# Batched matrix product on one core: the rounding to 16 bits moved to GpSimd, VectorE and ScalarE in loops, one output buffer per group

## The chip, the core and the metric

The kernel runs on one core of one Trainium2 chip. The metric is the device time of one execution in microseconds (us); lower is better. Each kernel is run several times and the median counts. Beside the times there is a profile: one execution recorded by the hardware profiler, with the start and length of each instruction on the engines TensorE (PE in the profile; its weight loads are PEld), VectorE (DVE), ScalarE (ACT), GpSimd (POOL) and SyncE (SP), and with the DMA transfers.

## What is computed

The reference is a batch of 32 independent matrix products in float32:

```
x: (32, 256, 512)   y: (32, 512, 384)   out: (32, 256, 384)
out = einsum('bij,bjk->bik', x, y)
```

x is 16.8 MB, y is 25.2 MB and the output is 12.6 MB, so 54.5 MB cross between the device memory and the core's SBUF.

## The kernel before

**Groups.** The 32 batches are worked through in N = 8 groups of Q = 4 batches. One DMA (`load_x`, lines 65 to 67) brings the four x of a group into `x_sb`: 32 partitions for each batch, 8 rows of 512 floats in each partition (16 KB). One DMA (`load_y`, lines 69 to 71) brings the four y into `y_sb`: again 32 partitions for each batch, 16 rows of 384 floats in each partition (24 KB). One DMA (`store`, lines 185 to 191) writes the output of a group. So a group has 5.24 MB of loads and 1.57 MB of stores. There are two buffers for x and three for y (lines 41 and 42).

**Rounding.** The products are made in float16. VectorE rounds x of a group in one instruction (`cast_x`, line 109, 4096 elements in each partition) into one of two `x_r` buffers, and y in four instructions of 1536 elements in each partition (`round_y`, line 124) into the single `y_r`.

**Transposes.** The products need x transposed. VectorE transposes pairs of float16 as if they were 32-bit words, in blocks of 32 by 32 (`transpose_x`, line 119). The output rows of a group are done in NE = 2 halves (e = 0 and 1), and the transposes of one half come in NC = 4 chunks, which go to the single buffer `xt_sb`. From group 6 on (`WIDE_GROUPS`) each chunk is two smaller transposes, and an output copy covers 64 partitions instead of 32.

**Products.** TensorE loops over groups and halves (lines 233 to 251). A half has T = 16 steps of four products, one for each batch of the group, each of 32 rows against 384 columns; the four batches use four row strips of the array and add up in four banks of PSUM, so there are eight banks for the two halves. TensorE waits for one `s_xt` mark for each chunk of four steps, and at the start of a half for the marks `s_act` and `s_dve`, which say that the banks have been copied out. `s_pe` counts what TensorE has finished: `chunk_done` is the mark of a chunk and `bank_done` that of a bank.

**Copies out of PSUM.** ScalarE copies seven of the eight banks of a group to SBUF and VectorE one, in pieces of 32 partitions (`collect`, line 137); in the last group they share the banks evenly. The outputs of groups 0 to 4 go to five `o_sb` buffers, those of groups 5 and 6 to the two halves of the third y buffer, and that of group 7 to the first `o_sb` buffer again, once the store of group 0 has landed (`s_first`).

**Order.** Each engine's order is written out by hand. VectorE does, for each group: the four transposes of half 1 (each after the chunk of half 0 is done), the rounding of the next x, then by turns a piece of the next y and a transpose of half 0 of the next group, then its copies. SyncE issues all DMAs, in program order, on one queue: y(0), x(0), y(1), x(1), then for n from 2 to 7 y(n) and x(n), and only then the eight stores (lines 193 to 204). y(n) waits until group n-3 has passed its half 0 (so that the third buffer back is free), x(n) until x(n-2) is rounded. Store n waits until the first chunk of half 1 of group n+1 is done; the last one waits for the last copies (`s_last`). GpSimd only clears semaphores at the end.

Of the kernel before, what the change touches and what calls it, by code (L numbers as in the profile page):

```python
# [8 lines left out]
MM_DT = mybir.dt.float16  # L9
F32 = mybir.dt.float32  # L10
P = 128
Q = 4
STEP = 4
WIDE_GROUPS = 6


@with_exitstack
def kernel(
# [6 lines left out]
    nc = tc.nc  # L25

    B, I, J = x.shape
    _, _, K = y.shape

    PQ = P // Q  # L30
    R = I // PQ
    T = J // PQ
    TW = T // 2
    NE = I // P
    N = B // Q
    NC = T // STEP

    def sbuf(name, shape, dtype):
        return nc.alloc_sbuf_tensor(name, shape, dtype).ap()

    x_sb = [sbuf(f"x_sb{i}", [P, R, J], F32) for i in range(2)]
    y_sb = [sbuf(f"y_sb{i}", [P, T, K], F32) for i in range(3)]
    o_sb = [sbuf(f"o_sb{i}", [P, R, K], F32) for i in range(5)]
    x_r = [sbuf(f"x_r{i}", [P, R, J], MM_DT) for i in range(2)]
    xt_sb = sbuf("xt_sb", [P, TW, P], F32)
    y_r = sbuf("y_r", [P, T, K], MM_DT)
    o_ps = nc.alloc_psum_tensor("o_ps", [P, NE * Q, 512], F32).ap()


    s_x = [nc.alloc_semaphore(f"s_x{n}") for n in range(N)]  # L50
    s_y = [nc.alloc_semaphore(f"s_y{n}") for n in range(N)]
    s_first = nc.alloc_semaphore("s_first")
    s_xt = nc.alloc_semaphore("s_xt")
    s_act = nc.alloc_semaphore("s_act")
    s_dve = nc.alloc_semaphore("s_dve")
    s_pe = nc.alloc_semaphore("s_pe")
    s_cast = nc.alloc_semaphore("s_cast")
    s_last = nc.alloc_semaphore("s_last")
    s_sp = nc.alloc_semaphore("s_sp")
    s_out = nc.alloc_semaphore("s_out")  # L60
    mine = s_x + s_y + [s_first, s_xt, s_act, s_dve, s_pe, s_cast, s_last, s_sp]
    nums = sorted(s.num for s in mine)
    assert nums == list(range(nums[0], nums[-1] + 1)) and s_out.num == nums[-1] + 1

    def load_x(n):
        src = x[n * Q : (n + 1) * Q].rearrange("g (p r) j -> (g p) r j", r=R)
        return nc.sync.dma_start(out=x_sb[n % 2], in_=src).then_inc(s_x[n], 16)

    def load_y(n):
        src = y[n * Q : (n + 1) * Q].rearrange("g (q t) k -> (g q) t k", t=T)  # L70
        return nc.sync.dma_start(out=y_sb[n % 3], in_=src).then_inc(s_y[n], 16)


    for ins in (load_y(0), load_x(0), load_y(1), load_x(1)):
        tc.no_tile_sem_insts.add(ins.ins.name)
    tc.close()
    tc.compile()  # L77


    MARKS = NC - 1 + Q  # L80

    def bank_done(n, e, g):
        return (n * NE + e) * MARKS + NC + g

    def chunk_done(n, e, a):
        return (n * NE + e) * MARKS + (a + 1 if a < NC - 1 else MARKS)

    def width(n):
        return PQ if n < WIDE_GROUPS else 2 * PQ

    def on_vector(n, e, g):
        if n < N - 1:
            return (e, g) == (NE - 1, Q - 1)
        return g % 2 == 1

    def o_of(n):
        if n in (5, 6):
            flat = y_sb[2].rearrange("p t k -> p (t k)")
            half = flat[:, (n - 5) * R * K : (n - 4) * R * K]
            return half.rearrange("p (r k) -> p r k", r=R)  # L100
        return o_sb[n % 5 if n < 5 else 0]


    v = nc.vector
    AW = STEP // 2

    def cast_x(n):
        v.wait_ge(s_x[n], 16)
        v.tensor_copy(x_r[n % 2], x_sb[n % 2]).then_inc(s_cast, 1)  # L109

    def transpose_x(n, e, a):
        b = width(n) // PQ
        src = x_r[n % 2].bitcast(F32).rearrange(
            "p (b h e) (q t) -> p b e t h q", b=b, e=NE, t=TW
        )
        dst = xt_sb.rearrange("p t (h s b) -> p b t h s", s=PQ, b=b)
        w = slice(a * AW, (a + 1) * AW)
        for c in range(b):
            ins = v.transpose(dst[:, c, w], src[:, c, e, w])  # L119
        ins.then_inc(s_xt, 1)  # L120

    def round_y(n, a):
        s = slice(a * STEP, (a + 1) * STEP)
        v.tensor_copy(y_r[:, s], y_sb[n % 3][:, s])  # L124

    def collect(n, eng, copy, vector, last):
        w = width(n)
        per = P // w
        o = o_of(n).rearrange("p (u f) k -> p u f k", u=Q // per)
        for e in range(NE):  # L130
            for g in range(Q):
                if on_vector(n, e, g) != vector:
                    continue
                eng.wait_ge(s_pe, bank_done(n, e, g))
                a = g % per * w
                for h in range(per):
                    ins = copy(  # L137
                        o[a : a + w, g // per, h * NE + e],
                        o_ps[h * w : (h + 1) * w, e * Q + g, :K],
                    )  # L140
                if (e, g) in last:
                    ins.then_inc(*last[e, g])


    v.sem_inc(s_dve, 3)
    v.wait_ge(s_y[0], 16)
    for a in range(NC):
        round_y(0, a)
    cast_x(0)
    v.wait_ge(s_cast, 1)  # L150
    for a in range(NC):
        transpose_x(0, 0, a)
    for n in range(N):
        for a in range(NC):
            v.wait_ge(s_pe, chunk_done(n, 0, a))
            transpose_x(n, 1, a)
        if n + 1 < N:
            cast_x(n + 1)
            v.wait_ge(s_y[n + 1], 16)
            for a in range(NC):  # L160
                v.wait_ge(s_pe, chunk_done(n, 1, a))
                round_y(n + 1, a)
                if a == 0:
                    v.wait_ge(s_cast, n + 2)
                transpose_x(n + 1, 0, a)
            collect(n, v, v.tensor_copy, True, {(NE - 1, Q - 1): (s_dve, 2)})
        else:
            v.wait_ge(s_first, 16)
            collect(n, v, v.tensor_copy, True, {(NE - 1, Q - 1): (s_last, 1)})


    a_ = nc.scalar
    a_.sem_inc(s_act, 2)
    for n in range(N):
        if n == N - 1:
            a_.wait_ge(s_first, 16)
            last = {(NE - 1, Q - 2): (s_last, 1)}
        else:
            last = {(0, Q - 1): (s_act, 1), (NE - 1, Q - 2): (s_act, 1)}
        collect(n, a_, a_.copy, False, last)  # L180


    sp = nc.sync

    def store(n):
        w = width(n)
        per = P // w
        dst = out[n * Q : (n + 1) * Q].rearrange("(u g) (s f) k -> (g s) u f k", g=per, s=w)
        sp.dma_start(
            out=dst, in_=o_of(n).rearrange("p (u f) k -> p u f k", u=Q // per)  # L190
        ).then_inc(s_first if n == 0 else s_out, 16)

    for n in range(2, N):
        if n >= 3:
            sp.wait_ge(s_pe, bank_done(n - 3, 0, Q - 1))
        load_y(n)
        sp.wait_ge(s_cast, n - 1)
        load_x(n)
    for n in range(N):
        if n < N - 1:  # L200
            sp.wait_ge(s_pe, chunk_done(n + 1, 1, 0))
        else:
            sp.wait_ge(s_last, 2)
        store(n)
    sp.sem_inc(s_sp, 1)
    sp.wait_op(s_out, 16 * (N - 1), "sem-ge").then_inc(s_out, -16 * (N - 1))


    nc.gpsimd.wait_ge(s_sp, 1)
    nc.gpsimd.sem_clear(range(nums[0], nums[-1] + 1))  # L210


    te = nc.tensor

    def take(sem):
        te.wait_op(sem, 1, "sem-ge").then_inc(sem, -1)  # L216
# [16 lines left out]
    with te.Fori(0, N):  # L233
        with te.Fori(0, NE) as e:
            take(s_act)
            take(s_dve)
            for t in range(T):
                if t % STEP == 0:
                    take(s_xt)
                for g in range(Q):  # L240
                    s = slice(g * PQ, (g + 1) * PQ)
                    ins = product(
                        o_ps[:, e * Q + g, :K],
                        xt[s, t // 2, :, t % 2],
                        y_r[s, t],
                        t == 0,
                        t == T - 1,
                        g,
                    )
                    if t == T - 1 or (g == Q - 1 and t % STEP == STEP - 1):  # L250
                        ins.then_inc(s_pe, 1)
# [30 lines left out]
```

## Time and profile before

| what | us |
|---|---|
| time, three runs | 132.65, 132.67, 132.85 |
| median | 132.67 |
| span of the profiled execution, first to last instruction | 131.3 |
| median less span (no time of its own is recorded for the profiled execution) | 1.37 |
| VectorE busy | 101.3 |
| ScalarE busy | 90.7 |
| TensorE busy | 65.3 |
| GpSimd busy | 0.2 |

The busy time of an engine is the sum over its instructions; the span is the longest that any of them could be busy. The page of the profile also cuts the span into 40 equal slices and gives for each slice the busy share of each engine, the clock granted to TensorE and the share in which the 16 DMA engines were busy. Other views of the same trace group the instructions by line and shape, list them in order of time, list who waited for whom, or give the busy times in windows that one chooses.

### The profile page before, as it was taken

To read this page: it belongs to the slowest core of one execution; us is meant where nothing else is said; L and a number is where in the kernel's file an instruction comes from. 1 tells how busy PE (TensorE), PEld (TensorE's weight loads), DVE (VectorE), ACT (ScalarE), POOL (GpSimd) and SP (SyncE) were. 2 spreads that over 40 slices of the span, in tenths; PEclk is the share of its full clock that TensorE was granted. 3 is DMA by queue.
4 is the path that set the end of the run, shared out by engine and by line. 5 is a ranking of instruction groups with operands and counts; after the bars stand their busy time and mean duration, and the time that the engine had idled before them with its cause. 6 is when DMAs were issued, how large, how long until landed. Compare 5 with 4: busy or idle time off the path is not lost. (4 is left out here: it accounts for less than half of the span.)

```text
span 131.3 us, 2703 instructions
## 1 busy us (share of the span) xinstructions
PE 65.3 (50%) x1024; PEld 50.7 (39%) x1024; DVE 101.3 (77%) x154; ACT 90.7 (69%) x191; POOL 0.2 (0%) x4
## 2 busy tenths in 40 slices
PE   0000019911959096708880799059814986665000
PEld 0000019900946063408750776059604953332000
DVE  0006596449999999999899969997999889999300
ACT  0300000699999999999999999999999999255000
POOL 0000000000000000000000000000000000000000
PEclk9999999996589977975698569955995599999655
DMA  5999999999999999999999999999999999999995
GB/s 135 434 419 419 452 442 409 424 457 427 409 462 427 422 414 457 419 414 414 464 427 402 437 452 427 412 444 434 417 412 421 419 430 427 434 427 426 412 423 217
DMA packets 3715, 54.55 MB, mean 415 GB/s; under 512 B 384, under 2 KB 384, under 8 KB 896
## 3 DMA queue, kind: packets, MB, share of 16 engines
q1 hardware_dynamic: 3712, 54.53, 97.9%
q14 instruction: 3, 0.02, 0.0%
HBM read 41.94 MB, written 12.58 MB: 415 GB/s over the span
## 5 line engine op out<-in xcount | busy, mean ns | idle before, releaser
L219 PE MATMUL o_ps<-y_r,xt_sb 32*128 32x384 f16 x1024 | 65.3, 396 | 54.5 <-PEq L216 53.5
L137 ACT COPY o_sb<-o_ps 32x384 f32<-32x384 f32 (+1 forms) x148 | 69.6, 471 | 26.5 <-PE o_ps L219 24.6
L219 PEld LDWEIGHTS o_ps<-y_r,xt_sb 32*128 32x128 f16 x1024 | 50.7, 111 | 68.8 <-issue 61.4
L119 DVE STREAM_TRANSPOSE xt_sb<-x_r 128x256 f32<-128x256 f32 (+1 forms) x80 | 39.7, 525 | 5.2 <-PE o_ps L219 5.0
L124 DVE CAST y_r<-y_sb 128x1536 f16<-128x1536 f32 x32 | 29.4, 927 | 11.1 <-DMA y_sb<-in_y_dram 11.1
L109 DVE CAST x_r<-x_sb 128x4096 f16<-128x4096 f32 x8 | 18.1, 2257 | 4.5 <-DMA x_sb<-in_x_dram 4.5
L137 ACT COPY y_sb<-o_ps 32x384 f32<-32x384 f32 (+1 forms) x42 | 19.8, 471 | 0.8
L137 DVE COPY o_sb<-o_ps 32x384 f32<-32x384 f32 (+1 forms) x28 | 15.6, 556 | 0.5
L137 ACT ACT_TABLE_LOAD x1 | 1.3, 1283 | 3.7 <-PEq L77 3.7
L137 DVE COPY y_sb<-o_ps 32x384 f32<-32x384 f32 (+1 forms) x6 | 3.3, 556 | 0.1
L266 POOL MEMSET const-bfloat16-1.0<- 128x1 bf16 x1 | 0.1, 102 | 0.0
L266 POOL MEMSET const-uint8-127<- 128x1 uint8 x1 | 0.1, 102 | 0.0
L266 POOL MEMSET const-float32-0.0<- 128x1 f32 x1 | 0.1, 99 | 0.2 <-issue 0.2
L266 POOL MEMSET const-float32-1.0<- 128x1 f32 x1 | 0.1, 99 | 0.0
## 6 DMA issues: line engine op xcount, KB each, us to landing
y_sb<-in_y_dram SPq DMA_DIRECT2D x8, 3072.0 KB, 21.5
x_sb<-in_x_dram SPq DMA_DIRECT2D x8, 2048.0 KB, 22.0
out_dram<-o_sb SPq DMA_DIRECT2D x6, 1536.0 KB, 26.6
out_dram<-y_sb SPq DMA_DIRECT2D x2, 1536.0 KB, 13.1
```

The source lines that it names most:

```text
L109: v.tensor_copy(x_r[n % 2], x_sb[n % 2]).then_inc(s_cast, 1)
L119: ins = v.transpose(dst[:, c, w], src[:, c, e, w])
L124: v.tensor_copy(y_r[:, s], y_sb[n % 3][:, s])
L137: ins = copy(o[a : a + w, g // per, h * NE + e], o_ps[h * w : (h + 1) * w, e * Q + g, :K],)
L219: return te.add_instruction(mybir.InstMatmult(name=nc.get_next_instruction_name(), start_tensor_calc=start, stop_tensor_calc=stop, tile_si ...
L266: nc = _bacc.Bacc("TRN2", target_bir_lowering=False, num_devices=1)
```

## The change

**Rounding.** GpSimd rounds all x (one instruction of 4096 elements in each partition) and all y (two instructions of 3072 elements, `PIECES` = 2). The single `x_r` buffer has room for one group; GpSimd waits for `s_free`, which VectorE raises after its first copy of half 0, before it overwrites it. A piece of y waits until TensorE has finished half 1 of the group before, up to the middle for the first piece and to the end for the second. TensorE waits for a mark `s_yr` before the first and the ninth step of each half.

**VectorE** keeps the transposes and takes bank 3 of each half (two banks of each group, four copies of 32 partitions each). It goes through seven groups in a hardware loop; the last group is written out. It waits for `s_words` (x of the next group is rounded) between half 0 and half 1.

**ScalarE** copies banks 0 to 2 of each half, in a double hardware loop.

**Buffers.** Each group has an output buffer of its own (`o_sb`, eight of 12 KB in each partition). y has two buffers instead of three. The wide transposes and copies of groups 6 and 7 are gone; all stores write 12 KB runs, where those of groups 6 and 7 wrote 6 KB runs.

**Loads.** x goes ahead of y in each group. x(n) waits until x(n-2) is rounded, y(n) until x(n-1) is rounded (by then GpSimd, which works in order, has also rounded y(n-2)). The stores still stand behind all loads in SyncE's order.

The core of the diff:

```diff
-    y_sb = [sbuf(f"y_sb{i}", [P, T, K], F32) for i in range(3)]
-    o_sb = [sbuf(f"o_sb{i}", [P, R, K], F32) for i in range(5)]
-    x_r = [sbuf(f"x_r{i}", [P, R, J], MM_DT) for i in range(2)]
+    y_sb = [sbuf(f"y_sb{i}", [P, T, K], F32) for i in range(2)]
+    o_sb = sbuf("o_sb", [P, N, NE, H, K], F32)
+    x_r = sbuf("x_r", [P, NE, H, J], MM_DT)
...
-    for ins in (load_y(0), load_x(0), load_y(1), load_x(1)):
+    for ins in (load_x(0), load_y(0), load_x(1), load_y(1)):
...
-    for n in range(2, N):
-        if n >= 3:
-            sp.wait_ge(s_pe, bank_done(n - 3, 0, Q - 1))
-        load_y(n)
-        sp.wait_ge(s_cast, n - 1)
-        load_x(n)
+    for n in range(2, N):
+        sp.wait_ge(s_cast, n - 1)
+        load_x(n)
+        sp.wait_ge(s_cast, n)
+        load_y(n)
...
+    po = nc.gpsimd
+    for n in range(N):
+        po.wait_ge(s_x[n], 16)
+        if n:
+            po.wait_ge(s_free, 2 * n - 1)
+        po.tensor_copy(
+            x_r.rearrange("p e h j -> p (e h) j"), x_sb[n % 2]
+        ).then_inc(s_cast, 1)
+        po.wait_ge(s_cast, n + 1)
+        po.sem_inc(s_words, 1)
+        po.wait_ge(s_y[n], 16)
+        for a in range(PIECES):
+            if n:
+                po.wait_ge(s_pe, chunk_done(n - 1, NE - 1, (a + 1) * NC // PIECES - 1))
+            s = slice(a * TY, (a + 1) * TY)
+            ins = po.tensor_copy(y_r[:, s], y_sb[n % 2][:, s])
+            ins.then_inc(s_yr, 1 if a < PIECES - 1 else 1 + PIECES)
...
+    with v.Fori(0, N - 1) as n:
+        for e in range(NE):
+            if e:
+                v.wait_op(s_words, 1, "sem-ge").then_inc(s_words, -1)
+            for a in range(NC):
+                v.wait_ge(s_pe, chunk_done(n, e, a))
+                transpose_x(1 - e, a)
+            collect(v, v.tensor_copy, n, e, Q - 1, s_free, s_dve)
...
+    with a_.Fori(0, N) as n:
+        with a_.Fori(0, NE) as e:
+            for g in range(Q - 1):
+                a_.wait_ge(s_pe, bank_done(n, e, g))
+                collect(a_, a_.copy, n, e, g, None, s_act if g == Q - 2 else None)
...
             for t in range(T):
+                if t % TY == 0:
+                    take(s_yr)
                 if t % STEP == 0:
                     take(s_xt)
```

More of the change, by code (lines that the diff above doesn't have):

```diff
@@ L12 @@
 Q = 4
+NE = 2
 STEP = 4
-WIDE_GROUPS = 6
+PIECES = 2
 @with_exitstack
@@ L31 @@
     R = I // PQ
+    H = R // NE
     T = J // PQ
     TW = T // 2
-    NE = I // P
     N = B // Q
     NC = T // STEP
+    TY = T // PIECES
     def sbuf(name, shape, dtype):
@@ L51 @@
     s_y = [nc.alloc_semaphore(f"s_y{n}") for n in range(N)]
-    s_first = nc.alloc_semaphore("s_first")
     s_xt = nc.alloc_semaphore("s_xt")
+    s_yr = nc.alloc_semaphore("s_yr")
+    s_cast = nc.alloc_semaphore("s_cast")
+    s_words = nc.alloc_semaphore("s_words")
+    s_free = nc.alloc_semaphore("s_free")
     s_act = nc.alloc_semaphore("s_act")
@@ L56 @@
     s_pe = nc.alloc_semaphore("s_pe")
-    s_cast = nc.alloc_semaphore("s_cast")
-    s_last = nc.alloc_semaphore("s_last")
     s_sp = nc.alloc_semaphore("s_sp")
     s_out = nc.alloc_semaphore("s_out")
-    mine = s_x + s_y + [s_first, s_xt, s_act, s_dve, s_pe, s_cast, s_last, s_sp]
+    mine = s_x + s_y + [s_xt, s_yr, s_cast, s_words, s_free, s_act, s_dve, s_pe, s_sp]
     nums = sorted(s.num for s in mine)
@@ L70, in load_y @@
         src = y[n * Q : (n + 1) * Q].rearrange("g (q t) k -> (g q) t k", t=T)
-        return nc.sync.dma_start(out=y_sb[n % 3], in_=src).then_inc(s_y[n], 16)
-    for ins in (load_y(0), load_x(0), load_y(1), load_x(1)):
+        return nc.sync.dma_start(out=y_sb[n % 2], in_=src).then_inc(s_y[n], 16)
+    for ins in (load_x(0), load_y(0), load_x(1), load_y(1)):
         tc.no_tile_sem_insts.add(ins.ins.name)
@@ L86, in chunk_done @@
         return (n * NE + e) * MARKS + (a + 1 if a < NC - 1 else MARKS)
-    def width(n):
-        return PQ if n < WIDE_GROUPS else 2 * PQ
-    def on_vector(n, e, g):
-        if n < N - 1:
[L93 to L101, printed above, removed]
+    sp = nc.sync
@@ new lines, in store @@
+    def store(n):
+        dst = out[n * Q : (n + 1) * Q].rearrange("g (s f) k -> (g s) f k", s=PQ)
+        src = o_sb[:, n].rearrange("p e h k -> p (e h) k")
+        sp.dma_start(out=dst, in_=src).then_inc(s_out, 16)
+    for n in range(2, N):
[4 more added lines that the diff above has]
+    for n in range(N):
+        if n < N - 1:
+            sp.wait_ge(s_pe, chunk_done(n + 1, NE - 1, 0))
+        else:
+            sp.wait_ge(s_act, NE)
+            sp.wait_ge(s_dve, NE)
+        store(n)
@@ new lines @@
+    sp.sem_inc(s_sp, 1)
+    sp.wait_op(s_out, 16 * N, "sem-ge").then_inc(s_out, -16 * N)
+    po = nc.gpsimd
+    for n in range(N):
+        po.wait_ge(s_x[n], 16)
[13 more added lines that the diff above has]
+            ins.then_inc(s_yr, 1 if a < PIECES - 1 else 1 + PIECES)
@@ L104 @@
+    po.wait_ge(s_sp, 1)
+    po.sem_clear(range(nums[0], nums[-1] + 1))
     v = nc.vector
     AW = STEP // 2
[L107 to L116, printed above, removed]
-        w = slice(a * AW, (a + 1) * AW)
-        for c in range(b):
-            ins = v.transpose(dst[:, c, w], src[:, c, e, w])
-        ins.then_inc(s_xt, 1)
@@ L122, in round_y @@
[L122 to L129, printed above, removed]
-        for e in range(NE):
[L131 to L142, printed above, removed]
@@ L145 @@
-    v.sem_inc(s_dve, 3)
-    v.wait_ge(s_y[0], 16)
-    for a in range(NC):
[L148 to L169, printed above, removed]
@@ L172 @@
-    a_ = nc.scalar
[L173 to L191, printed above, removed]
@@ L193 @@
-    for n in range(2, N):
-        if n >= 3:
-            sp.wait_ge(s_pe, bank_done(n - 3, 0, Q - 1))
-        load_y(n)
-        sp.wait_ge(s_cast, n - 1)
-        load_x(n)
[L199 to L210, printed above, removed]
+    words = x_r.bitcast(F32).rearrange("p e h (q t) -> p e t h q", t=TW)
@@ new lines, with transpose_x, collect @@
+    xt_w = xt_sb.rearrange("p t (h s) -> p t h s", s=PQ)
+    def transpose_x(e, a):
+        w = slice(a * AW, (a + 1) * AW)
+        v.transpose(xt_w[:, w], words[:, e, w]).then_inc(s_xt, 1)
+    def collect(eng, copy, n, e, g, first=None, last=None):
+        for h in range(H):
+            ins = copy(
+                o_sb[g * PQ : (g + 1) * PQ, n, e, h],
+                o_ps[h * PQ : (h + 1) * PQ, e * Q + g, :K],
+            )
+            if h == 0 and first is not None:
+                ins.then_inc(first, 1)
+            if h == H - 1 and last is not None:
+                ins.then_inc(last, 1)
@@ new lines @@
+    v.sem_inc(s_dve, NE)
+    v.wait_op(s_words, 1, "sem-ge").then_inc(s_words, -1)
+    for a in range(NC):
+        transpose_x(0, a)
+    with v.Fori(0, N - 1) as n:
+        for e in range(NE):
+            if e:
+                v.wait_op(s_words, 1, "sem-ge").then_inc(s_words, -1)
+            for a in range(NC):
+                v.wait_ge(s_pe, chunk_done(n, e, a))
+                transpose_x(1 - e, a)
+            collect(v, v.tensor_copy, n, e, Q - 1, s_free, s_dve)
+    for a in range(NC):
+        v.wait_ge(s_pe, chunk_done(N - 1, 0, a))
+        transpose_x(1, a)
@@ L213 @@
+    collect(v, v.tensor_copy, N - 1, 0, Q - 1, None, s_dve)
+    v.wait_ge(s_pe, chunk_done(N - 1, 1, NC - 1))
+    collect(v, v.tensor_copy, N - 1, 1, Q - 1, None, s_dve)
+    a_ = nc.scalar
+    a_.sem_inc(s_act, NE)
+    with a_.Fori(0, N) as n:
[3 more added lines that the diff above has]
+                collect(a_, a_.copy, n, e, g, None, s_act if g == Q - 2 else None)
     te = nc.tensor
```

## The prediction

> **What bounds the kernel now.** I read the page's DMA lines first, since 54.5 MB have to move whatever the engines do.
>
> ```profile
> span 131.3 us, 2703 instructions
> ...
> PE 65.3 (50%) x1024; PEld 50.7 (39%) x1024; DVE 101.3 (77%) x154; ACT 90.7 (69%) x191; POOL 0.2 (0%) x4
> ...
> DMA  5999999999999999999999999999999999999995
> ...
> q1 hardware_dynamic: 3712, 54.53, 97.9%
> ```
>
> No engine fills the span, but the 16 DMA engines do: 97.9% of 131.3 us is 128.5 us, so 54.53 MB move at 424.4 GB/s. The line of 40 slices has no gap between the first and the last slice. The kernel is bound by its transfers, and what the engines do matters only where it leaves the queue empty. The windows show both ends of the stream (columns: busy time and count on PE, PEld, DVE, ACT, POOL, then granted clock, DMA share, GB/s):
>
> ```profile
> 4.00:16.00 12.00, 0.00 (x0) 0.00 (x0) 3.61 (x5) 0.94 (x1) 0.00 (x0) 1.00 1.01 435
> 16.00:28.00 12.00, 7.65 (x128) 7.16 (x128) 7.00 (x9) 3.77 (x8) 0.00 (x0) 1.00 1.00 431
> ...
> 107.00:119.00 12.00, 8.32 (x169) 4.93 (x164) 11.88 (x25) 7.19 (x16) 0.00 (x0) 1.00 1.01 428
> 119.00:127.00 8.00, 0.87 (x21) 0.36 (x12) 3.59 (x7) 1.90 (x4) 0.00 (x0) 0.72 1.00 420
> 127.00:131.30 4.30, 0.00 (x0) 0.00 (x0) 0.00 (x0) 0.00 (x0) 0.00 (x0) 0.50 0.64 267
> ```
>
> The last window is 64% busy: transfers end at about 127 + 0.64 x 4.3 = 129.8 us, 1.5 us before the end of the span, and so begin at about 129.8 - 128.5 = 1.3 us. Next the timeline, for why the queue never runs dry:
>
> ```profile
> 0.73 0.39 SPq L71 DMA_DIRECT2D y_sb<-in_y_dram  x1
> ...
> 11.06 3.57 DVE L124 CAST y_r<-y_sb 128x1536 f16<-128x1536 f32 x4 [11.06 <-DMA y_sb<-in_y_dram]
> 15.95 2.29 DVE L109 CAST x_r<-x_sb 128x4096 f16<-128x4096 f32 x1 [1.32 <-DMA x_sb<-in_x_dram]
> ...
> 79.08 2.24 DVE L109 CAST x_r<-x_sb 128x4096 f16<-128x4096 f32 x1
> ...
> 81.36 0.33 SPq L67 DMA_DIRECT2D x_sb<-in_x_dram  x1
> ...
> 92.71 2.25 DVE L109 CAST x_r<-x_sb 128x4096 f16<-128x4096 f32 x1
> ...
> 122.70 0.38 SPq L189 DMA_DIRECT2D out_dram<-o_sb  x1
> ```
>
> A group's loads (5.243 MB) take 12.35 us at 424.4 GB/s, but the casts of x at 79.08 and 92.71 are 13.63 us apart: the engines are already slower than the loads. It costs nothing, because with three y buffers the last load is issued at 81.36, right behind the cast of x(5), with 41.94 MB less 34.0 MB (80.1 us by 0.4244) still to move, nearly 19 us of queue, and the stores follow at once. The last store is issued at 122.70 behind a queue that is still full.
>
> **What the change does to the stream.** It moves the same bytes. SyncE now issues y(n) behind the cast of x(n-1) on GpSimd, one group later than before, and behind that wait stand all later loads and all stores. Had GpSimd kept the old pace, the cast of x(6) would end at 92.71 + 2.25 = 95.0, while the queue would be through x(7) at 1.3 + 7 x 12.35 + 4.94 = 92.7: already a gap. So the pace of the engines now decides, and I work it out.
>
> **The chain of one group.** `x_r` and `y_r` are single. From the end of TensorE's half 0 of group n the order is forced: VectorE's last transpose of half 1, its first copy (which raises `s_free`), GpSimd's cast of x(n+1), its two pieces of y(n+1) in line behind it, then TensorE's second half-phase for half 0 of group n+1. Their rows, by shape (busy us, mean ns):
>
> ```profile
> L137 ACT COPY o_sb<-o_ps 32x384 f32<-32x384 f32 x140 | 65.8, 470 | 21.1 <-PE o_ps L219 19.2
> ...
> L124 DVE CAST y_r<-y_sb 128x1536 f16<-128x1536 f32 x32 | 29.4, 927 | 11.1 <-DMA y_sb<-in_y_dram 11.1
> L119 DVE STREAM_TRANSPOSE xt_sb<-x_r 128x256 f32<-128x256 f32 x48 | 29.1, 623 | 4.5 <-PE o_ps L219 4.3
> L109 DVE CAST x_r<-x_sb 128x4096 f16<-128x4096 f32 x8 | 18.1, 2257 | 4.5 <-DMA x_sb<-in_x_dram 4.5
> ...
> L137 DVE COPY o_sb<-o_ps 32x384 f32<-32x384 f32 x20 | 11.1, 556 | 0.4
> ```
>
> *GpSimd's casts* are shown nowhere; GpSimd has four tiny fills and nothing else. Between its two shapes VectorE's cast costs (2257 - 927) / (4096 - 1536) = 0.52 ns per element, plus 129 ns per instruction. That is the low end. The high end is VectorE's copy taken whole, 556 / 384 = 1.45 ns. Less those 129 ns it is 1.11, and ScalarE's copy is (470 - 129) / 384 = 0.89 ns. I take 0.89, an estimate: a cast there is again one input, one output and no arithmetic on an engine of its own, and ScalarE's is the row nearest to that. Then x costs 4096 x 0.89 + 129 = 3.77 us and a piece of y 3072 x 0.89 + 129 = 2.86 us.
>
> [...]
>
> *TensorE* has two speeds:
>
> ```profile
> 59.49 5.38 PE L219 MATMUL o_ps<-y_r,xt_sb 32*128 32x384 f16 x64 [4.56 <-PEq L216]
> ...
> 65.29 3.17 PE L219 MATMUL o_ps<-y_r,xt_sb 32*128 32x384 f16 x64 [0.42 <-PEq L216]
> ```
>
> ```profile
> 59.40:60.40 1.00, 0.91 (x11) 0.50 1.04 442
> ...
> 63.40:64.40 1.00, 1.00 (x20) 0.50 1.03 442
> 64.40:65.20 0.80, 0.47 (x10) 0.98 1.07 461
> ```
>
> After an idle time of 4.56 us the 64 products of a half take 5.38 us, at a granted clock of 0.50 until the end; the next half, 0.42 us behind it, takes 3.17. In the changed kernel TensorE idles longer still, about 8 us from the end of half 1 to the first piece of y, so I charge 2.69 us for each half-phase of half 0. A handoff costs about 0.12 us:
>
> ```profile
> 112.34 0.68 DVE L119 STREAM_TRANSPOSE xt_sb<-x_r 128x128 f32<-128x128 f32 x2
> ...
> 113.14 0.47 PEld L219 LDWEIGHTS o_ps<-y_r,xt_sb 32*128 32x128 f16 x16 [0.97 <-issue]
> ```
>
> (113.14 less 112.34 + 0.68.) **Sum of one period:** 0.62 + 0.56 + 3.77 + 2 x 2.86 + 2.69 + 4 x 0.12 = 13.84 us.
>
> **What is hidden, and by what.** VectorE's wait for the rounded x holds up the four transposes of the next half 0 and, behind them, its copies of half 1. The cast ends 0.12 + 0.62 + 0.56 + 0.12 + 3.77 = 5.2 us into the period; the four transposes end at 7.7, before the first piece of y (8.2), and the copies at about 10, before TensorE wants that bank again at 14.2. So VectorE costs nothing beyond its two terms; if it lost 0.5 us there, the period would grow by that. ScalarE has 24 copies instead of 28; its row
>
> ```profile
> 39.60 46.47 ACT L137 COPY o_sb<-o_ps 32x384 f32<-32x384 f32 x96
> ```
>
> gives 0.484 us each, 11.6 us a group, also inside the period, so the four copies it loses gain nothing there. The rounding taken off VectorE (2.26 + 4 x 0.93 = 6.0 us a group) gains nothing either: VectorE did not set the end, the transfers did. The loops add register work that the trace does not show; I take 0, bounded by one handoff (0.12 us) at each of the two VectorE steps in the chain, 2 us over eight groups. Loading x ahead of y changes nothing at the start: TensorE needs both, and both have landed at 15.95 in either order.
>
> **The sum.** The first y is rounded from 15.95 to 21.7; half 0 of group 0 ends at 21.7 + 0.12 + 2.69 = 24.5. Seven periods later, at 24.5 + 96.9 = 121.4, half 0 of group 7 ends. ScalarE then has 24 copies (half 1, over by 121.4 + 0.4 + 3.2 = 125.0, hides behind the first twelve): 121.4 + 11.6 = 133.0. The queue: y(7) is issued when x(6) is cast, 24.5 + 5 x 13.84 + 5.2 = 98.9, starts about 0.6 us later (0.73 to 1.3 at the start), takes 7.4 and is through at 106.9; seven stores of 1.573 MB, 3.7 us each, then end at 132.8. So the last store finds an empty queue: 133.0 + 0.6 + 3.7 + 1.5 for landing = 138.8 us of span. Against the profiled span of 131.3, and with the 1.37 us between that span and the median of 132.67 added, this is **140.2 us**, 7.5 us more. Each 0.1 ns per element moves it by 0.1 x (7 x 10.24 + 6.1) = 7.8 us.
>
> **The rivals.**
>
> *The transfers stay the bound, and the kernel gets a little faster.* The period falls to the loads' 12.35 us at (12.35 - 13.84) / 10.24 + 0.89 = 0.74 ns per element, or at 0.85 if TensorE's second half-phase already runs at the full clock (1.6 us instead of 2.69). Then the queue never empties, and the 12 KB runs of the last two stores could lift the 428 and 420 GB/s of the windows from 107 to 127 towards the 431 of the early ones: 8.50 MB in 19.7 instead of 20.0 us, so 132.4 us; without that effect 132.7. For it speaks VectorE's 0.52 ns; against it that every other copy shown costs 0.89 or more.
>
> *GpSimd is clearly slower and everything waits for it.* At VectorE's 1.11 ns the sum is 140.2 + 17 = 157, at its 1.45 it is 184. For it speaks that GpSimd has 81,920 elements per partition to round, so even a small difference is large; and that GpSimd would then be busy nearly the whole span, with the last load issued at 98.9 plus 13 to 34 us. [...]
>
> *The rounding leaves VectorE but GpSimd and VectorE get in each other's way.* Beside the casts VectorE has 8 transposes and 8 copies a group, 9.4 us. If half of that were added to the period, it would be 18.5 us and the time about 175. Nothing in the trace shows them working together; it would read as casts of unequal length.
>
> **How the numbers follow.** Forecast, 0.8 to 1.0 ns (134 to 149 us): 0.48. Transfers bound: 0.15. Slower GpSimd, 149 to 184 us: 0.24; beyond 184: 0.08. Interference: 0.05, inside the same span. A measurement of this kernel tells about 0.2% (0.27 us) from no change. Of the 0.15 I give 0.09 to faster (132.4 and below) and 0.06 to no change; slower has 0.85. The range runs from 132.4 to 184: it leaves out the 0.08 above and a few hundredths below.
>
> **What would show it.** Right: casts on GpSimd of about 3.8 and 2.9 us; starts of x casts 13.8 us apart from group 2 on; gaps in the DMA line from about 45 us on, and none once the stores run; TensorE idle about 8 us a group, at clock 0.50 in half 0; the last load issued near 99 us; span near 139. Wrong: a DMA line without gaps (casts under 0.74 ns); casts above 1.1 ns; ScalarE's copies or VectorE's transposes as the last releaser of TensorE, instead of GpSimd's second piece of y; casts whose length follows what VectorE does.

## The result and the profile after

The changed kernel takes 144.88 us (median of 4 runs, 144.77 to 145.04), the kernel before 132.74 us beside it: 1.0913 times as long, 95% interval 1.09 to 1.0926, or 12.1 us more. The forecast was 140.2 us, 7.5 us more. The sign and the range held; 4.7 us were missing. Medians here and below are over all runs; ratios leave out runs more than 1.5% above the fastest of their kernel.

The page of the changed kernel: first the span and the engines, then the line of the DMA engines over 40 slices, then the queue.

```profile
span 143.3 us, 3259 instructions
...
PE 73.1 (51%) x1024; PEld 57.1 (40%) x1024; DVE 74.3 (52%) x128; ACT 110.7 (77%) x208; POOL 72.5 (51%) x28
...
DMA  5999999999998999799899998988898999999637
...
q1 hardware_dynamic: 3456, 54.53, 92.9%
```

The same bytes move, but the line now has slices of 7 and 8 from before the middle on, and a hole near the end. VectorE has lost 27 us of work and GpSimd has gained 72. ScalarE, which copies 24 pieces a group where it copied 28, has 20 us more. The groups of instructions say why (busy us, mean ns; then the idle time before them):

```profile
L147 ACT COPY o_sb<-o_ps x192 | 90.2, 470 | 2.3
...
L119 POOL CAST x_r<-x_sb 128x4096 f16<-128x4096 f32 x8 | 28.8, 3600 | 40.1 <-DVE o_sb L147 32.0
L129 POOL CAST y_r<-y_sb 128x3072 f16<-128x3072 f32 x16 | 43.5, 2747 | 6.2 <-DMA y_sb<-in_y_dram 3.7
L147 ACT ACT_TABLE_LOAD x16 | 20.5, 1283 | 24.9 <-PE o_ps L189 24.7
```

There is an ACT_TABLE_LOAD for each of the 16 halves, 1.283 us each. The kernel before has one in all, off to the side at its start (3.66 us):

```profile
L137 ACT ACT_TABLE_LOAD x1 | 1.3, 1283 | 3.7 <-PEq L77 3.7
```

The load stands inside ScalarE's hardware loop, so each turn runs it. ScalarE's timeline and TensorE's, side by side:

```profile
60.06 1.28 ACT L147 ACT_TABLE_LOAD   x1
61.35 5.77 ACT L147 COPY o_sb<-o_ps  x12
67.14 1.28 ACT L147 ACT_TABLE_LOAD   x1
68.43 5.76 ACT L147 COPY o_sb<-o_ps  x12
74.21 1.28 ACT L147 ACT_TABLE_LOAD   x1
```

```profile
60.89 5.31 PE L189 MATMUL o_ps<-y_r,xt_sb 32*128 32x384 f16 x64 [3.97 <-PEq L186]
67.87 4.85 PE L189 MATMUL o_ps<-y_r,xt_sb 32*128 32x384 f16 x64 [1.67 <-PEq L186]
74.95 4.85 PE L189 MATMUL o_ps<-y_r,xt_sb 32*128 32x384 f16 x64 [2.23 <-PEq L186]
82.03 4.89 PE L189 MATMUL o_ps<-y_r,xt_sb 32*128 32x384 f16 x64 [2.23 <-PEq L186]
```

A half takes ScalarE 7.08 us without an idle moment, and from 60.89 us TensorE's halves start at that same distance (6.98, 7.08, 7.08), about 0.75 us after ScalarE has finished with the banks. Of the 7.08 us the copies take 5.77 and the load 1.28, which leaves 0.03. The number of loads follows the loop in the experiments below: eight with the loop over groups alone, one with both written out.

The end is ScalarE's too. SyncE issues its last load at 98.97 (98.9 forecast), the store of group 6 at 125.73, and the last store at 137.92, when ScalarE's last copy ends:

```profile
98.97 0.33 SPq L73 DMA_DIRECT2D y_sb<-in_y_dram  x1
...
125.73 0.33 SPq L96 DMA_DIRECT2D out_dram<-o_sb  x1
137.92 0.33 SPq L96 DMA_DIRECT2D out_dram<-o_sb  x1
```

The window before it (length, granted clock, DMA share, GB/s) shows that the queue had run out and waited for that store, which landed 5.4 us after its issue:

```profile
134.00:138.00 4.00, 0.50 0.29 123
```

### The profile page after: what moved, and what is told of

It is laid out like the page before. It is cut to its first block, busy times and chain, and to the rows that moved or that the text cites. A ratio compares the mean times of both kernels' runs of the same rounds, so it can differ in the third digit from the quotient of the medians.

```text
span 143.3 us, 3259 instructions
## 1 busy us (share of the span) xinstructions
PE 73.1 (51%) x1024; PEld 57.1 (40%) x1024; DVE 74.3 (52%) x128; ACT 110.7 (77%) x208; POOL 72.5 (51%) x28
## 5 line engine op out<-in xcount | busy, mean ns | idle before, releaser
L189 PE MATMUL o_ps<-y_r,xt_sb 32*128 32x384 f16 x1024 | 73.1, 437 | 54.6 <-PEq L186 53.7
L147 ACT COPY o_sb<-o_ps x192 | 90.2, 470 | 2.3
L189 PEld LDWEIGHTS o_ps<-y_r,xt_sb 32*128 32x128 f16 x1024 | 57.1, 121 | 70.1 <-issue 60.8
L143 DVE STREAM_TRANSPOSE xt_sb<-x_r 128x256 f32<-128x256 f32 x64 | 38.7, 630 | 52.7 <-PE o_ps L189 26.5
L119 POOL CAST x_r<-x_sb 128x4096 f16<-128x4096 f32 x8 | 28.8, 3600 | 40.1 <-DVE o_sb L147 32.0
L129 POOL CAST y_r<-y_sb 128x3072 f16<-128x3072 f32 x16 | 43.5, 2747 | 6.2 <-DMA y_sb<-in_y_dram 3.7
L147 ACT ACT_TABLE_LOAD x16 | 20.5, 1283 | 24.9 <-PE o_ps L189 24.7
L147 DVE COPY o_sb<-o_ps 32x384 f32 (+1 forms) x64 | 35.6, 556 | 3.0 <-PE o_ps L189 1.6
```

The source lines that it names most:

```text
L119: po.tensor_copy(x_r.rearrange("p e h j -> p (e h) j"), x_sb[n % 2]).then_inc(s_cast, 1)
L129: ins = po.tensor_copy(y_r[:, s], y_sb[n % 2][:, s])
L143: v.transpose(xt_w[:, w], words[:, e, w]).then_inc(s_xt, 1)
L147: ins = copy(o_sb[g * PQ : (g + 1) * PQ, n, e, h], o_ps[h * PQ : (h + 1) * PQ, e * Q + g, :K],)
L189: return te.add_instruction(mybir.InstMatmult(name=nc.get_next_instruction_name(), start_tensor_calc=start, stop_tensor_calc=stop, tile_si ...
```

## The experiments

The theory after the traces: two chains run side by side at nearly the same pace, ScalarE's copies with their table loads (14.15 us a group) and GpSimd's chain through the single buffer of rounded x (13.7 us), and behind both lie loads that are issued too late. The rivals: that GpSimd's chain sets everything and the table loads cost only in the tail; that the gaps in the loads set the end. Ratios below are to the kernel before on the same chip. The two controls and the kernel with 6 KB runs were timed on a second chip, the other experiments on one.

**ScalarE's loops written out.**

```diff
-    with a_.Fori(0, N) as n:
-        with a_.Fori(0, NE) as e:
+    for n in range(N):
+        for e in range(NE):
```

> Only change to the changed kernel: ScalarE's two hardware loops are written out, so that the table load of 1.28 us, which stands inside the loop and runs 16 times, runs once. Theory (ScalarE's 7.08 us per half, table load included, set the pace from group 2 on; without the loads the chain through GpSimd, 13.7 us a group, does): half 0 of group 7 ends at about 24.7 + 7 x 13.7 = 120.6 us, ScalarE ends 11.6 us later, the store lands 5.4 us after that, 137.6 us of span, about 139 us. Rival A (the chain through GpSimd set the pace all along, the loads cost only in the last 24 copies): 141.5 to 142. Rival B (gaps in the load stream set the end): 144.9, no change.

Measured: 141.72 us, ratio 1.0664 (1.0594 to 1.0733). The pace is as the theory had it; the end is not. ScalarE's timeline, GpSimd's waits and the last store:

```profile
92.68 11.55 ACT L147 COPY o_sb<-o_ps 32x384 f32<-32x384 f32 x24 [2.11 <-PE o_ps L189]
106.32 11.56 ACT L147 COPY o_sb<-o_ps 32x384 f32<-32x384 f32 x24 [2.08 <-PE o_ps L189]
119.96 11.55 ACT L147 COPY o_sb<-o_ps 32x384 f32<-32x384 f32 x24 [2.09 <-PE o_ps L189]
```

```profile
POOL x_r L119 <- DVE o_sb L147: 30.9, 7, 4.5
```

```profile
131.54 0.33 SPq L96 DMA_DIRECT2D out_dram<-o_sb  x1
```

ScalarE now waits 2.1 us for TensorE in each group, so it no longer sets the pace, and GpSimd's x casts start 13.7 us apart, each after waiting for VectorE's first copy. ScalarE is done at 131.5, 6.4 us earlier. But the store then issued ends with the span at 140.8: it has a queue before it. Two windows of the DMA (length, granted clock, DMA share, GB/s):

```profile
98.00:110.00 12.00, 0.72 0.94 326
```

```profile
134.00:138.00 4.00, 0.50 0.89 377
```

So of 6.4 us gained on ScalarE only 3.2 reached the time (the profiled execution itself took 142.40 us), because the late loads were next in line. Rival A named 141.5 to 142 and hit the number, but for a reason that the trace refutes: TensorE's last half 0 ended earlier, too, at 120 instead of 123 us.

**Half the table loads.** Only the loop over groups is kept, the two halves are written out.

> Only change to the changed kernel: ScalarE's inner loop over the two halves is written out, the outer one over groups stays, so the table load runs 8 times instead of 16. Theory: ScalarE needs 11.55 + 1.3 = 12.9 us a group, less than the 13.7 of the chain through GpSimd, so the loads cost only in the tail: 120.6 + 12.9 (or 11.6 if the load falls before half 0 ends) + 5.4 = 137.6 to 138.9 us of span, 139 to 140.5 us. If the loads cost in proportion to their number instead: half of what writing out both loops gains, about 142.

Measured: 140.01 us (median of five runs, 138.96 to 143.41), ratio 1.051 (1.0463 to 1.0558). The theory's 139 to 140.5 holds: eight loads cost no more than one. The profiled execution is the longest of the five, 143.41 us; even there ScalarE still waits for TensorE, 0.8 to 1.2 us in each group:

```profile
107.28 1.28 ACT L147 ACT_TABLE_LOAD   x1 [0.83 <-PE o_ps L189]
108.57 11.55 ACT L147 COPY o_sb<-o_ps 32x384 f32 x24
```

The price is therefore not in proportion to the loads. That it begins where ScalarE's group passes the other chain's 13.7 us fits these runs, but none lies between 12.9 and 14.15 us to show it. That this kernel came out under the one with a single load isn't explained; its runs spread over 4.5 us and those of the other over 1.9, and this may be no more than that.

**A third y buffer, ScalarE's loops kept.**

```diff
+    y_sb.append(o_sb[:, N - 2 :].rearrange("p n e h k -> p (n e h) k"))
...
-        return nc.sync.dma_start(out=y_sb[n % 2], in_=src).then_inc(s_y[n], 16)
+        return nc.sync.dma_start(out=y_sb[n % 3], in_=src).then_inc(s_y[n], 16)
...
-        sp.wait_ge(s_cast, n)
         load_y(n)
```

> Change to the changed kernel: a third y buffer, which lies over the output buffers of groups 6 and 7 (not yet in use while y goes through it); y(n) is issued right behind x(n), one group earlier. ScalarE's loops stay. Theory (ScalarE sets the end, the gaps in the stream of transfers follow from that and cost nothing by themselves): 144.5 to 144.9. Rival B (the gaps set the end): the 10.2 us of idle DMA time shrink to about 3, so 137.5.

Measured: 144.17 us, ratio 1.0866 (1.0829 to 1.0903). The loads run without a break, and it gains 0.7 us, 0.3 more than the theory allowed: ScalarE still needs 14.15 us a group, and its last copies end at 137.3 us instead of 137.9. Its DMA line shows the break moved behind the stores that were ready:

```profile
DMA  5999999999999999999999999999999999272036
```

**Both.**

> Both: ScalarE's loops written out and the third y buffer. Theory (with ScalarE out of the way the chain through GpSimd sets the end, and the queue of transfers ends only a little ahead of it): 137.5 to 139, at most 1.5 us under the kernel with the loops written out alone. Rival B (behind ScalarE the late loads are what costs): 132.5 to 134.

Measured: 137.51 us (median of five runs, 137.13 to 139.83), ratio 1.0338 (1.0317 to 1.0359). The theory's number holds, its bound of 1.5 us does not: beside the kernel with the loops written out the third buffer is worth 4.2 us, beside the kernel with the loops 0.7. It could gain only once ScalarE was out of the way. Rival B's 132.5 to 134 fails. What remains is GpSimd's chain and, behind its last half 0, ScalarE's 24 copies: the DMA engines are nearly idle for eight microseconds before the last store is issued at 132.75 (the profiled execution took 139.83 us, 2.3 more than the median):

```profile
126.00:130.00 4.00, 0.69 0.14 58
130.00:134.00 4.00, 0.50 0.12 49
```

```profile
132.75 0.33 SPq L97 DMA_DIRECT2D out_dram<-o_sb  x1
```

**Two buffers for the rounded x.** ScalarE's and VectorE's loops are written out, group 7's output goes into the first y buffer to make room. y still has two buffers and GpSimd still rounds everything.

```diff
-    x_r = sbuf("x_r", [P, NE, H, J], MM_DT)
+    x_r = [sbuf(f"x_r{i}", [P, NE, H, J], MM_DT) for i in range(2)]
...
-        if n:
-            po.wait_ge(s_free, 2 * n - 1)
+        if n > 1:
+            po.wait_ge(s_free, 2 * n - 3)
```

> The changed kernel with ScalarE's and VectorE's loops written out and two buffers for the rounded x, so that GpSimd rounds the next x right behind y without waiting for VectorE's transposes (group 7's output goes to the first y buffer to make room). GpSimd still rounds everything, y still has two buffers. Theory (the chain through the single buffer of rounded x costs the rest): the period falls to the 12.35 us of the loads, ScalarE's 11.6 is below that: 132.2 to 133. Rival C (GpSimd's 9.1 us of casts a group beside its handoffs are too slow by themselves): 138 to 139, as with ScalarE's loops written out alone.

Measured: 132.51 us (11 runs), ratio 0.9981 (0.9972 to 0.999). All of the loss is gone, and the transfers bound the kernel again. GpSimd now waits only for data, and the queue is full to the end:

```profile
q1 hardware_dynamic: 3456, 54.53, 98.0%
```

```profile
POOL y_r L134 <- DMA y_sb<-in_y_dram: 26.8, 8, 3.7
```

```profile
82.78 3.60 POOL L124 CAST x_r<-x_sb 128x4096 f16<-128x4096 f32 x1
89.60 5.44 POOL L134 CAST y_r<-y_sb 128x3072 f16<-128x3072 f32 x2 [3.22 <-DMA y_sb<-in_y_dram]
94.99 3.60 POOL L124 CAST x_r<-x_sb 128x4096 f16<-128x4096 f32 x1
```

The x casts are 12.2 us apart: each follows the y before it at once, and the next y waits 3.2 us for its transfer. This also releases y(n) earlier, since its issue hangs on the cast of x(n-1). Rival C falls: 9.0 us of casts a group fit into 12.35 us.

**Control: one buffer of rounded x, all loops written out.**

> Control for the kernel with two buffers of rounded x: ScalarE's and VectorE's loops written out and group 7's output in the first y buffer, but one buffer of rounded x as in the changed kernel. Theory (the second buffer of rounded x is what brought the time to 132.5): 140.5 to 142.5, as with ScalarE's loops written out alone. Rival (VectorE's loop was the cost): 132.5 to 134.

Measured: 141.67 us, ratio 1.0694 (1.0645 to 1.0744), the same as with ScalarE's loops alone written out. VectorE's loop and the place of group 7's output cost nothing that shows; the second buffer did it.

**Control: two buffers of rounded x, ScalarE's loop kept.**

> The kernel with two buffers of rounded x, but with ScalarE's double loop back for groups 0 to 6 (group 7 written out), so that the table load runs 14 times. Theory (ScalarE's 14.15 us a group set the pace by themselves, whatever the chain through GpSimd does): from 23.5 us seven groups of 14.15 and one of 11.55 end at 134.1, the store lands 5.4 us later, 139.5 us of span, about 141 us. Rival (the single buffer of rounded x was the cost, the table loads only added to it): 132.5 to 134.

Measured: 141.73 us, ratio 1.0652 (1.0629 to 1.0676). The theory's number holds and the rival falls. From group 2 on GpSimd waits for nothing but TensorE, and each half of TensorE starts 0.75 us after ScalarE's copies:

```profile
POOL y_r L134 <- PE o_ps L198: 31.8, 6, 5.8
```

```profile
82.66 5.78 ACT L152 COPY o_sb<-o_ps  x12
88.45 1.28 ACT L152 ACT_TABLE_LOAD   x1
```

```profile
89.19 4.85 PE L198 MATMUL o_ps<-y_r,xt_sb 32*128 32x384 f16 x64 [2.22 <-PEq L195]
96.28 4.85 PE L198 MATMUL o_ps<-y_r,xt_sb 32*128 32x384 f16 x64 [2.24 <-PEq L195]
```

The halves start 7.09 us apart. So the single buffer of rounded x with the late loads behind it costs 9 us alone, and so do 14 table loads alone; both causes together cost 12. The two do not add up, and the comparison is not quite even: this kernel lacks the two loads of group 7, which stand in ScalarE's tail. With 2 x 1.28 us for them it would take about 144.3 us, an estimate, so that all 16 loads alone would account for nearly the whole loss.

**All of it: loops written out, two buffers of rounded x, three of y.**

> As the kernel with two buffers of rounded x, and the third y buffer as well (over the outputs of groups 5 and 6). Theory: the transfers bound it, so no gain over two buffers of rounded x alone beyond 0.3 us: 132.2 to 132.9; 12 KB runs in all stores may give up to 0.3 us against the kernel before. If late loads still cost in the kernel with two buffers of rounded x, this one is faster than it by that much.

Measured: 132.46 us (10 runs), ratio 0.9977 (0.9967 to 0.9986). The third y buffer adds nothing once the casts of x run early.

**The kernel before with two y buffers.**

```diff
-    y_sb = [sbuf(f"y_sb{i}", [P, T, K], F32) for i in range(3)]
-    o_sb = [sbuf(f"o_sb{i}", [P, R, K], F32) for i in range(5)]
+    y_sb = [sbuf(f"y_sb{i}", [P, T, K], F32) for i in range(2)]
+    o_sb = [sbuf(f"o_sb{i}", [P, R, K], F32) for i in range(7)]
...
-        if n >= 3:
-            sp.wait_ge(s_pe, bank_done(n - 3, 0, Q - 1))
+        sp.wait_ge(s_pe, bank_done(n - 2, 0, Q - 1))
```

> The kernel before with two y buffers instead of three (seven output buffers, so that no output lies in a y buffer); y(n) then waits until half 0 of group n-2 is done. Theory (at VectorE's own pace the lost buffer already leaves a gap): y(7) is issued at about 92 instead of 78.5 us, the queue is through x(6) at 87.8, so about 5 us of gaps: 136.5 to 138. Rival (the stores fill such gaps): 132.7.

Measured: 140.87 us (median of four runs, 139.47 to 142.05), ratio 1.0555 (1.0504 to 1.0606). The direction is right and the size too small by 3 to 4 us. y(7) was issued at 92.94, as forecast; but the GB/s of the 40 slices show that the loss is spread over the groups from 38 us on: slices of 317 to 361 GB/s recur, and one of 249 stands at 106 us:

```profile
GB/s 148 422 429 418 458 422 429 460 408 418 422 317 382 394 434 321 359 432 392 350 429 404 340 385 429 418 357 361 436 394 249 426 436 426 429 428 433 407 424 197
```

**6 KB runs in all stores**, as two stores a group, on the kernel with two buffers of rounded x.

> The kernel with two buffers of rounded x, each store cut into two of 6 KB runs (16 stores in place of 8, twice the packets in all groups). If 6 KB runs cost what the windows of the kernel before suggest (420 to 428 against 431 GB/s), 12.58 MB of stores take 0.2 to 0.8 us longer: 132.7 to 133.3. Rival (run length does not matter here, the gain of 0.3 us over the kernel before is from elsewhere): 132.4 to 132.6.

Measured: 132.79 us (12 runs), ratio 0.9999 (0.9989 to 1.0008), against 0.9981 (0.9972 to 0.999) with 12 KB runs. That is 0.2 to 0.3 us, at the low end of the expectation, and the intervals just touch. Twice as many stores were issued as well, and the two kernels ran on different chips, so run length may be the cause of the small gain over the kernel before, but is not shown to be.

## Why the prediction was right, and where it was short

*The transfers bound the kernel before, and fewer buffers expose the engines*: right. Taking one y buffer from the kernel before costs 7 to 8 us by itself; a second buffer of rounded x, with the loops written out, brings the changed kernel to 132.5.

*GpSimd's casts at 0.89 ns per element and 129 ns each*: 3.77 and 2.86 us forecast, 3.60 and 2.75 measured. From the two shapes, (3600 - 2747) / 1024 = 0.83 ns per element and 188 ns for each cast.

*The period of 13.84 us*: x casts in the changed kernel start 13.85 us apart on average (26.16 to 109.26 in six periods), and 13.68 with ScalarE's loops written out (25.78 to 107.83). The first agreement is luck: from the second half of group 3 on (67.87 us) ScalarE set the pace, and TensorE's halves 0 start 14.06 us apart on average (19.05 to 117.46 in seven periods). The prediction had listed ScalarE's copies as the last releaser of TensorE among the signs of being wrong, and that sign appeared. The chain that the forecast described is the second number. One part of its working was off without consequence: with ScalarE's loops written out TensorE idles 5.8 us before half 0, not about 8 (the forecast's own terms give 8.2 - 0.4 - 3.2 = 4.6), and half 0 is at half the clock all the same (it starts at 101.22 us; granted clock 0.50 in the windows from 100 to 104 us and 0.55 from 104 to 106).

*ScalarE's 24 copies take 11.6 us a group and hide inside the period; the loops cost at most a handoff*: this step failed. The copies take 11.55 us, but with a table load for each half ScalarE needs 14.15 us. It cost twice: TensorE reached the end of the last half 0 at 123.2 instead of 121.4, and ScalarE's tail behind that took 14.7 us instead of 11.6. The landing took 5.4 us instead of 5.8, and 1.6 us lay around the span instead of 1.4: 1.8 + 3.1 - 0.4 + 0.2 = 4.7 us, the whole of what was missing. The price was there to read: the page of the kernel before has one ACT_TABLE_LOAD of 1283 ns. That a loop's body would hold one, no earlier trace showed; I had priced the loops on VectorE alone.

*The queue ends at 132.8, just ahead of the last copies*: the issue of y(7) was right to 0.1 us in the changed kernel (97.82 without the table loads, so this too is partly luck), but the transfers behind the gaps were taken at the full rate. With ScalarE's loops written out the window from 98 to 110 us moves 326 GB/s instead of 424, 1.2 MB or 2.8 us less, and the queue, not ScalarE, ends last. Without the table loads the forecast would thus have been 1.5 us short, for this reason.

*The rivals.* A transfer-bound kernel did not come about: at 0.83 ns per element the casts stayed above the 0.74 that the forecast had named for it, and the period has 4.6 us beside the casts. With a second buffer of rounded x the same casts were fast enough. The slower GpSimd did not either. Nor the interference: the eight casts of x take 3597 to 3601 ns and the sixteen of y 2747 or 2748 ns, though VectorE copies and transposes beside some of them and not beside others.

## What to carry to other kernels

Before work on ScalarE goes into a hardware loop, look for a table load in the instruction list and where it would land: 1.28 us is small once and large sixteen times (20.5 us of ScalarE's time in the changed kernel). Here a single buffer between two engines turned their times into a sum, 13.7 us a group where two buffers had 12.2; doubling it (8 KB in each partition here) was worth 9 us once the table loads were out of the loop, where moving 6 us a group to an idle engine gained at most 0.3 us. When a kernel is bound by its transfers, count how far ahead the loads are issued: in the kernel before, nearly 19 us of queue (an estimate from the 7.9 MB of loads left at 81.36 us, at 424.4 GB/s) hid engines that took 13.63 us a group. The change spent that slack and showed them all at once, so that removing one of them gained little until the next was removed too: 3.2 us without the table loads, 0.7 with the third y buffer, 7.4 with both.

## What the runs showed of the hardware

In the changed kernel the queue did not run at its full rate at once when it was refilled: behind the load issued at 43.70 us the windows 44 to 46, 46 to 48 and 48 to 50 us have 201, 369 and 430 GB/s, with the DMA engines 82, 87 and 101% busy. The windows from 36 to 60 us have DMA engines 92 and 93% busy at 369 and 376 GB/s, while the two windows before them, from 12 to 36 us, have 437 and 433 with the engines fully busy (1.02 and 1.01). By the busy share that is 401 and 404 GB/s against 428 and 429: packets took longer as well as being fewer. What slows them was not settled. GpSimd's casts of x repeated to 4 ns in 3600 (3597 to 3601 ns). TensorE needed 5.3 to 5.5 us for the 64 products of a half after idle times of 4 to 6 us (the halves that start at 33.19, 47.10 and 60.89 us), as in the kernel before (5.2 to 5.5 us after 4.6 to 5.6 us). While the halves of the changed kernel came every 7.08 us (67.87 to 110.33 us, with 1.7 to 2.5 us of idle time between them), each took 4.5 to 4.9 us, and the fast half of 3.2 us was gone. Even spacing alone does not do that: with the third y buffer and ScalarE's loops, halves that start at 95.58, 102.71 and 109.74 us take 3.21, 5.69 and 3.17 us. What decides between the two was not settled.
